# Two transformer blocks on one core: loads, norms and splits placed beside the stage before

## The chip, the core and the metric

The kernel runs on one core of one Trainium2 chip. TensorE (PE) multiplies, with its weight loads shown as PEld; VectorE (DVE), ScalarE (ACT) and GpSimd (POOL) do the elementwise work; SP issues most DMAs, POOL some. The metric is the device time of one execution in microseconds.

## What is computed

The reference takes x of [1, 2048, 1024] in float32 through two blocks.

- Block 1: norm, one input projection, a Fourier branch and grouped-query attention over 16 meta and 2048 other tokens, an output projection, a residual and a norm.
- Block 2: norm; an input projection to 256 + 128 + 32 + 512 + 512 + 8 columns (the compressed query, the compressed key and value, a rope key, the mLSTM's two streams, its gates); an 8-head attention whose queries, keys and values come from the compressed ones by up-projections, with rotary cos and sin on 32 dimensions; an mLSTM in chunks whose input and forget gates run through scans over the sequence; an output projection and residual. Then 32 experts of width 256, two per token out of one group, and an embedding term:

```
y = experts(u) ; x = x + w0*y0 + w1*y1
x = x + sigmoid(norm(x) @ w_ple_gate) * (p @ w_ple) ; out = norm(x)
```

## The kernel before

Every product is made in float32 accuracy from two rounded halves: `split` writes hi on ScalarE (line 73, or 76 with a scale) and lo = raw - hi on VectorE (74, 77) or GpSimd, and `mm3` issues three matmuls, hi x hi (line 83), lo x hi (84), hi x lo (85). The instruction order on each engine is fixed when the kernel is built: it follows the order in which the code issues the work, and each engine runs its list in order. SP's queue, too, runs in order: an issue that waits holds all behind it.

The stages are generators: `e.beside(gen)` in one stage runs the next part of another, up to its `yield`, on the other side of the memory (`e.flip` changes sides).

- `phase_d`, `project_out`: out projection of block 1 in 16 tiles of 128 tokens. `post` in it does the norm.
- `phase_e`: input projection of block 2 in 8 groups of 256 tokens. The weights are in two parts, th/tl (424 columns, 8 splits, loads at lines 848 and 849) and fh/fl (1024 columns, 16 splits in `load_split`, 256 KB each, loads at line 710, three buffers `ws`). `prep(g)` loads, norms, transposes (878) and splits the tokens; products go to `pm`, the th ones first.
- `phase_f`: up-projections in 4 groups of 512 tokens. Each group loads cos and sin (`cs`) and its rope key (`kr`), and the next group's inputs (`xf`, in `load`), makes eight products for the queries, stores QNT and QRT, four for the keys (KNT) and four for the values (V). `put` copies results out of PSUM. `gates` (from line 1380 on) is called at its start: `ig`, `fg` loaded, a chain of VectorE instructions, columns stored to memory and loaded back in another shape (COL, DC), and three transposes on PE at its end.
- `phase_k`: 32 experts. `block(x, second)` is built twice behind a test of the expert's count: with a second pass (`hidden2`, over 64 rows) or without. `hidden` makes eight steps of gate and up products into `g`, one PSUM tile; at each step `beside(k)` puts other work in. `out_a` transposes the activations of the expert before, sg, into ah and al, `out_b` multiplies them by the down weights dh/dl and scatters y to memory. RG and RD are the raw tiles of the up and gate, and of the down weights; `split_in` and `split_down` make halves for expert x + 3 and load the raw tiles again.
- `embed`: the product of p with w_ple (wq, and xq for p), stored as PP, for 13 tiles earlier and, here, for the last 3.
- `phase_l`: the last stage: for 16 tiles load x, yy (two expert results) and pp, add, norm, gate product `pg`, sigmoid, norm, store. The gate's weights lie raw in `raw[0]`, `raw[1]` (2 MB each) and are split to wgh/wgl when the experts are done.

Of the kernel before, what the change touches and what calls it, by code (L numbers as in the profile page):

```python
# [10 lines left out]
F32 = mybir.dt.float32  # L11
# [781 lines left out]
def phase_d(e):  # L793

    nc, d = e.nc, e.d
    MIXT = e.scratch("MIXT", [1024, S])
    X1 = e.scratch("X1", [S, D])

    def post(wk, sm, pt, gb):
        def run(t, r, y):  # L800
            if t == 16:
                return
            ss = sm.tile([128, 1], F32, name="ss")
            junk = wk.tile([128, D], BF, name="junk", bufs=1)
            nc.scalar.activation(junk, y, AF.Square, accum_out=ss)
            rstd(e, sm, ss, D)
            nc.vector.scalar_tensor_tensor(y, y, ss, gb, op0=ALU.mult, op1=ALU.mult)
            nc.sync.dma_start(X1[r, :], y)
        return run

    yield from project_out(e, MIXT, d["w_out"][0], d["x"][0], d["final_g"], "d_", post, False)


def phase_e(e, then):

# [10 lines left out]
    with ExitStack() as st:  # L826
# [3 lines left out]
        ut = pool("e_ut", 2)  # L830
        wk = pool("e_wk", 2)
        wt = pool("e_wt", 1)
        sm = pool("e_sm", 4)
        wp = pool("e_w", 1)
        pt = pool("e_pt", 2, space=PSUM)
        pm = pool("e_pm", 3, space=PSUM)
# [14 lines left out]
        fh, fl = load_split(e, wp, ld, w_in, 1024, 1024, "f", gcol, 416)  # L851
# [3 lines left out]
        taps = cst.tile([128, 4, 5], F32, name="taps")  # L855
        for k in range(4):
            nc.sync.dma_start(taps[:, :, k], d["conv_w_2"][0, k].rearrange("(h p) -> p h", p=128))
        nc.sync.dma_start(taps[:, :, 4], d["conv_b_2"][0].rearrange("(h p) -> p h", p=128))
        xms = [cst.tile([128, 4, 3 + GB], F32, name=f"xm{i}") for i in range(2)]
        nc.gpsimd.memset(xms[0][:, :, :3], 0.0)  # L860

        def prep(g):
            hi = ut.tile([128, 8, GB], F32R, name="uhi")
            lo = ut.tile([128, 8, GB], F32R, name="ulo")
            for i in range(GB // 128):
                t = g * (GB // 128) + i
                xt = ld.tile([128, D], F32, name="xt", bufs=2)
                nc.sync.dma_start(xt, X1[t * 128:(t + 1) * 128, :])
                ss = sm.tile([128, 1], F32, name="ss")
                junk = wk.tile([128, D], BF, name="junk", bufs=1)  # L870
# [11 lines left out]
        prep(0)  # L882
        pend = []

# [15 lines left out]
        for g in range(NG):  # L900
# [5 lines left out]
            for i in range(GB // 128):  # L906
# [6 lines left out]
                junk = wk.tile([128, D], BF, name="junk", bufs=1)  # L913
# [80 lines left out]
def phase_f(e, then):  # L994
# [16 lines left out]
    with ExitStack() as st:  # L1011
# [38 lines left out]
        yield  # L1050
        gates(e, pool)
        xp.append(pool("f_x1", 1))
        ld = pool("f_ld", 2)
        wk = pool("f_wk", 2)
        ps = pool("f_ps", 6, space=PSUM)
        e.stage = ld
        for g in range(S // GB):
            c = slice(g * GB, (g + 1) * GB)
            cs = ld.tile([128, 2, GB], F32, name="cs")
            for i, T in enumerate((CT, ST)):  # L1060
                nc.sync.dma_start(cs[:, i, :], bass.AP(tensor=T.tensor, offset=T.offset + g * GB, ap=[[0, 4], [S, 32], [1, GB]]))
            kr = ld.tile([64, GB], F32, name="kr")
            nc.sync.dma_start(kr, KRW[:, c])
# [7 lines left out]
            nc.sync.dma_start(KRT[:, c], ko[:, 0])  # L1071
# [25 lines left out]
            nc.sync.dma_start(rows(QRT), r)  # L1097
            e.beside(then)
# [801 lines left out]
def embed(e, tiles, side, late=None):  # L1900
# [7 lines left out]
    with ExitStack() as st:  # L1908
# [26 lines left out]
        yield  # L1935
# [13 lines left out]
        x = turn(tiles[0])  # L1949
        for t in tiles:  # L1950
            if t + 3 in tiles:
                load(t + 3)
            (h, l), x = x, turn(t + 1) if t + 1 in tiles else None
            y = wk.tile([128, D], F32, name="y")
            for j in range(2):
                o = slice(j * 512, (j + 1) * 512)
                q = pm.tile([128, 512], F32, name="q", bufs=2)
                for k in range(2):
                    mm3(e, q, (h[:, k], l[:, k]), (w[0][:, k, o], w[1][:, k, o]), k == 0, k == 1)
                nc.scalar.activation(y[:, o], q, AF.Copy)  # L1960
            nc.sync.dma_start(PP[t * 128:(t + 1) * 128, :], y)
            yield
# [23 lines left out]
def phase_k(e, last):  # L1986
# [11 lines left out]
    with ExitStack() as st:  # L1998
# [4 lines left out]
        std, op = far("k_sd", 1), far("k_y", 2)  # L2003
# [21 lines left out]

        def split_in(w, s, x):
# [200 lines left out]
        def block(x, second):  # L2227
# [4 lines left out]
            if x:  # L2232
                a = out_a(SG[x - 1])
# [4 lines left out]
            a2 = []  # L2238

            def beside(k):  # L2240
                if k in TURN and x < 31:
# [36 lines left out]
TURN, OUT2, TURN2 = (0, 2), 6, (4, 5)  # L2278


def phase_l(e, tiles):
# [11 lines left out]
    with ExitStack() as st:  # L2293
# [5 lines left out]
        wq = wp.tile([128, 2, 1024], F32, name="wq")  # L2299
        nc.sync.dma_start(wq, d["w_ple_2"][0].rearrange("(k p) c -> p k c", p=128))  # L2300
        xq = wp.tile([128, len(tiles), 256], F32, name="xq")
        nc.sync.dma_start(xq, d["p_2"][0, 0, tiles.start * 128:tiles.stop * 128].rearrange("(t p) c -> p t c", p=128))
        e.late = wq, xq
# [13 lines left out]
        wg = next(parts)  # L2317
        for _ in parts:
            yield
        ld = pool("l_ld", 2)  # L2320
        wk = pool("l_wk", 2)
# [4 lines left out]
        def head(t):  # L2326
# [3 lines left out]
            if x is None:  # L2330
                x = ld.tile([128, D], F32, name="x", bufs=4)
# [27 lines left out]
        for t in range(16):  # L2359
# [3 lines left out]
            pp = ld.tile([128, D], F32, name="pp")  # L2363
# [10 lines left out]
            sg = wk.tile([128, D], F32, name="sg")  # L2374
# [15 lines left out]
def body(e):  # L2390
    tc = e.tc
    with tc.tile_pool(name="consts", bufs=1) as cp:
# [9 lines left out]
        for _ in phase_d(e):  # L2402
            pass
        e.flip()
        with ExitStack() as st:
# [5 lines left out]
            phase_e(e, heads)  # L2411
# [10 lines left out]
            last = phase_l(e, range(LATE, 16))  # L2422
            phase_k(e, last)
            rest = embed(e, range(LATE, 16), "left", e.late)
            e.beside(rest)
            next(last)
            e.flip()
            for _ in rest:
                pass
            e.flip()  # L2430
# [25 lines left out]
```

## Time and profile before

| what | value |
|---|---|
| median of 3 runs | 3594.97 us (3589.45 to 3596.04) |
| the profiled execution | 3607.51 us, of which its span 3605.8 us |
| mean granted clock of PE | 0.966 |
| PE busy | 3364.2 us (93%), 16556 matmuls |
| VectorE, ScalarE, GpSimd busy | 2448.4, 2052.4, 696.2 us |
| bytes moved | 468.82 MB, 130 GB/s |

The stages around the change, by the first and last matmul of each in the trace:

| stage | from, to (us) |
|---|---|
| out projection of block 1 (`phase_d`) | 1337 to 1529.5 |
| input projection of block 2 (`phase_e`) | 1529.5 to 1827.8 |
| up-projections and gates (`phase_f`) | 1827.8 to 1928.5 |
| experts (`phase_k`) | 2893 to 3374 |
| last stage (`phase_l`) | 3400.6 to 3606 |

Blocks of an expert with a second pass follow one another at 16.2 us, those without (eight of them, 3026 to 3130) at 13.

The profile is one execution on the hardware. A row of the timeline names the engine, the line of the kernel, the tile written and the tiles read, and in square brackets how long the engine stood before it and what ended that. A row of the waits says which engine stood before which line, and for what. [...]

### The profile page before, as it was taken

To read this page: it belongs to the slowest core of one execution; us is meant where nothing else is said; L and a number is where in the kernel's file an instruction comes from. 1 tells how busy PE (TensorE), PEld (TensorE's weight loads), DVE (VectorE), ACT (ScalarE), POOL (GpSimd) and SP (SyncE) were. 2 spreads that over 40 slices of the span, in tenths; PEclk is the share of its full clock that TensorE was granted. 3 is DMA by queue.
4 is the path that set the end of the run, shared out by engine and by line. 5 is a ranking of instruction groups with operands and counts; after the bars stand their busy time and mean duration, and the time that the engine had idled before them with its cause. 6 is when DMAs were issued, how large, how long until landed. Compare 5 with 4: busy or idle time off the path is not lost. (4 is left out here: it accounts for less than half of the span.)

```text
span 3605.8 us, 48799 instructions
## 1 busy us (share of the span) xinstructions
PE 3364.2 (93%) x16556; PEld 2611.3 (72%) x16557; DVE 2448.4 (68%) x4612; ACT 2052.4 (57%) x3660; POOL 696.2 (19%) x729
## 2 busy tenths in 40 slices
PE   8999999999999999989986889989999989899798
PEld 6787766666666657789975667777788766677587
DVE  5835667888888854464365777877856568878554
ACT  4442357887777872253223777877833367677433
POOL 0000000000000010000032333332200046665332
PEclk9999999999999999999997999999999989899899
DMA  5333322111112035353247433322355678888753
GB/s 157 102 121 101 97 70 72 46 31 50 43 32 57 11 91 179 121 153 109 74 148 173 93 77 74 81 69 59 88 174 157 222 260 305 319 301 307 256 189 132
DMA packets 313432, 468.82 MB, mean 130 GB/s; under 512 B 66263, under 2 KB 201192, under 8 KB 304864
## 3 DMA queue, kind: packets, MB, share of 16 engines
q1 hardware_dynamic: 293622, 404.26, 36.9%
q0 software_dynamic: 19520, 60.97, 4.6%
q8 instruction: 148, 2.42, 0.3%
q14 instruction: 142, 1.16, 0.1%
HBM read 333.81 MB, written 135.24 MB: 130 GB/s over the span
## 5 line engine op out<-in xcount | busy, mean ns | idle before, releaser
L588 DVE TENSOR_TENSOR pl<-pe,ph 128x1024 fp32r<-128x1024 f32 (+1 forms) x272 | 340.6, 1253 | 89.0 <-ACT ph L581 87.7
L519 DVE TENSOR_REDUCE mx<-pmx 128x1 f32<-128x512 f32 x512 | 344.2, 684 | 82.9 <-PE pmx L518 76.5
L579 ACT ACTIVATE pe<-ps 128x1024 f32<-128x1024 f32 (+1 forms) x272 | 278.5, 1025 | 146.2 <-PE ps L577 135.9
L581 ACT ACTIVATE ph<-pe 128x1024 fp32r<-128x1024 f32 (+1 forms) x272 | 287.4, 1058 | 7.4
L74 DVE TENSOR_TENSOR gl<-raw,gh 128x512 fp32r<-128x512 f32 x256 | 235.2, 960 | 15.0 <-ACT gh L73 12.6
L576 PE MATMUL ps<-t,kh 128*128 128x512 f32 (+1 forms) x544 | 239.0, 439 | 0.5 <-ACT pe L579 0.5
L1280 DVE TENSOR_TENSOR pl<-pe,ph 128x512 fp32r<-128x512 f32 (+1 forms) x320 | 210.7, 662 | 40.5 <-ACT ph L1273 38.0
L577 PE MATMUL ps<-t,kl 65*128 65x512 f32 (+1 forms) x544 | 222.3, 409 | 0.0
L602 PE MATMUL acc<-ph,vh 128*65 128x512 f32 (+1 forms) x544 | 217.1, 399 | 0.0
L604 PE MATMUL acc<-pl,vh 128*65 128x512 f32 (+1 forms) x544 | 214.9, 395 | 0.0
L603 PE MATMUL acc<-ph,vl 128*65 128x512 f32 (+1 forms) x544 | 214.7, 395 | 0.0
L518 PE MATMUL pmx<-kh,t 128*128 128x512 f32 x512 | 207.1, 410 | 1.9 <-DVE mx L519 1.1
L1244 DVE TENSOR_REDUCE mx<-pmx 128x1 f32<-128x512 f32 (+2 forms) x320 | 190.7, 598 | 13.0 <-PE pmx L1243 12.6
L1271 ACT ACTIVATE pe<-ps 128x512 f32<-128x512 f32 (+1 forms) x320 | 166.9, 524 | 43.5 <-PE ps L1269 40.5
L74 POOL TENSOR_TENSOR dl<-sd,dh 128x512 fp32r<-128x512 f32 x128 | 172.8, 1371 | 71.6 <-ACT dh L73 69.2
L1273 ACT ACTIVATE ph<-pe 128x512 fp32r<-128x512 f32 (+1 forms) x320 | 179.5, 564 | 6.5
L1267 PE MATMUL ps<-t,kh 113*128 113x512 f32 (+1 forms) x320 | 138.0, 431 | 38.8 <-ACT pe L1271 29.8
L73 ACT ACTIVATE gh<-raw 128x512 fp32r<-128x512 f32 x256 | 143.4, 625 | 12.4 <-PE p L85 9.4
L83 PE MATMUL pm<-uhi,fh 128*128 128x256 f32 x512 | 145.3, 285 | 3.7 <-ACT fh L76 2.0
L84 PE MATMUL pm<-ulo,fh 128*128 128x256 f32 x512 | 143.6, 282 | 0.0
L85 PE MATMUL pm<-uhi,fl 128*128 128x256 f32 x512 | 143.2, 283 | 0.3 <-DVE fl L77 0.3
L788 DVE TENSOR_TENSOR y<-p,xt 128x1024 f32<-128x1024 f32 x32 | 39.2, 1224 | 152.9 <-PE p L85 151.2
(539 smaller groups left out, 9672.9 us busy)
## 6 DMA issues: line engine op xcount, KB each, us to landing
raw<-in_w_gate_e SPq DMA_DIRECT2D x32, 1024.0 KB
raw<-in_w_up_e SPq DMA_DIRECT2D x32, 1024.0 KB
sd<-in_w_down_e SPq DMA_DIRECT2D x32, 1024.0 KB
ws<-in_w_in SPq DMA_DIRECT2D x80, 256.0 KB
xt<-in_x SPq DMA_DIRECT2D x32, 512.0 KB
scr_X<-y SPq DMA_DIRECT2D x32, 512.0 KB
xt<-scr_X SPq DMA_DIRECT2D x32, 512.0 KB
yy<-scr_Y POOLq DMA_DIRECT2D x32, 512.0 KB, 5.0
```

Source lines behind the costliest of these rows:

```text
L74: (eng or nc.vector).tensor_tensor(lo, src, f32(hi), op=ALU.subtract)
L518: nc.tensor.matmul(p, t1[:, i * 128:(i + 1) * 128], kh[:, j * 512:(j + 1) * 512], start=True, stop=True)
L519: nc.vector.reduce_max(mx[:, i, j:j + 1], p, axis=AX.X)
L576: nc.tensor.matmul(p[:n, c], kh[:, k0:k0 + n], t1[:, c], start=True, stop=False)
L577: nc.tensor.matmul(p[:n, c], kl[:, k0:k0 + n], t2[:, c], start=False, stop=True)
L579: nc.scalar.activation(pe[:n], p[:n], AF.Exp, scale=0.125)
L581: nc.scalar.activation(ph[:n], pe[:n], AF.Copy)
L588: nc.vector.tensor_tensor(pl[:n], pe[:n], f32(ph[:n]), op=ALU.subtract)
L602: nc.tensor.matmul(A[u][j], vh[:n, i, :65], ph[:n, c], start=i == 0, stop=False)
L603: nc.tensor.matmul(A[u][j], vl[:n, i, :65], ph[:n, c], start=False, stop=False)
L604: nc.tensor.matmul(A[u][j], vh[:n, i, :65], pl[:n, c], start=False, stop=i == 16)
L1280: nc.vector.tensor_tensor(pl[:, c0:], pe[:, c0:], f32(ph[:, c0:]), op=ALU.subtract)
```

## The change

It has four parts.

1. `phase_e` becomes a generator, and its first part (th/tl, the loads, norm, transposes and splits of group 0) is run beside `phase_d` from its tile 13 on (`NEXT`); its loads stand among the first tiles. The fh/fl weights, the taps and the memory they need come behind it.
2. `phase_f` loads cos and sin for all 2048 tokens (`cst`) and the rope key (`krw`) once, in 18 DMAs, ahead of `gates`. The three buffers of `wk` become more (2 to 3), `put` gives VectorE the first of four results and ScalarE three, and KRT is stored behind QRT.
3. In `phase_k`, `out_a` of the expert before moves from the block's start to hidden's step 4 (`OUT`), the second pass' from step 6 to 7, its token transposes from 4 and 5 to 3 and 6.
4. The raw weights of the late `embed` are loaded into the down weights' raw tiles when their last use is done (`load_late`), and no longer into a tile of `phase_l`. `embed` makes its first transposes ahead of its `yield`. In `phase_l`, x, pp and sg lie in quarters of the gate's raw tiles.

```diff
-def phase_d(e):
+def phase_d(e, then):
         def run(t, r, y):
+            if t == NEXT:
+                e.beside(then)
...
+NEXT = 13
 def phase_e(e, then):
-        ut = pool("e_ut", 2)
+        ut = [pool("e_u0", 1)]
...
-        fh, fl = load_split(e, wp, ld, w_in, 1024, 1024, "f", gcol, 416)
...
         prep(0)
+        yield
+        wp = pool("e_w", 1)
+        ut.append(pool("e_u1", 1))
+        wk = pool("e_wk", 2)
+        pm = pool("e_pm", 3, space=PSUM)
+        fh, fl = load_split(e, wp, ld, w_in, 1024, 1024, "f", gcol, 416)
+        taps = wp.tile([128, 4, 5], F32, name="taps")
...
 def phase_f
+        cst = wt.tile([128, 2, S], F32, name="cst")
+        krw = wt.tile([64, S], F32, name="krw")
+        for c in (slice(0, GB), slice(GB, S)):
+            for r in range(4):
+                for i, T in enumerate((CT, ST)):
+                    nc.sync.dma_start(cst[r * 32:(r + 1) * 32, i, c], T[:, c])
+            nc.sync.dma_start(krw[:, c], KRW[:, c])
         gates(e, pool)
-        wk = pool("f_wk", 2)
+        wk = pool("f_wk", 3)
         for g in range(S // GB):
-            cs = ld.tile([128, 2, GB], F32, name="cs")
-            for i, T in enumerate((CT, ST)):
-                nc.sync.dma_start(cs[:, i, :], bass.AP(tensor=T.tensor, offset=T.offset + g * GB, ap=[[0, 4], [S, 32], [1, GB]]))
-            kr = ld.tile([64, GB], F32, name="kr")
-            nc.sync.dma_start(kr, KRW[:, c])
+            cs, kr = cst[:, :, c], krw[:, c]
-            nc.sync.dma_start(KRT[:, c], ko[:, 0])
             def put(o, p, i):
-                if i % 2:
+                if i:
...
             nc.sync.dma_start(rows(QRT), r)
+            nc.sync.dma_start(KRT[:, c], ko[:, 0])
 def embed
-        yield
+        if not late:
+            yield
...
         x = turn(tiles[0])
+        if late:
+            yield
-def phase_k(e, last):
+def phase_k(e, last, keep, tiles):
+        wq = RD[0].rearrange("p (k a) c -> p k (a c)", k=2)
+        xq = RD[1].rearrange("p k c -> p (k c)")[:, :len(tiles) * 256].rearrange("p (t c) -> p t c", c=256)
+        e.late = wq, xq
+        def load_late(i):
...
                     if k == i == 1 and x < 32:
                         load_down(x, s)
+                    elif k == i == 1:
+                        load_late(x % 2)
...
-            if x:
-                a = out_a(SG[x - 1])
             parts(2)
...
             def beside(k):
+                if k == OUT and x:
+                    a.extend(out_a(SG[x - 1]))
-TURN, OUT2, TURN2 = (0, 2), 6, (4, 5)
+OUT, TURN, OUT2, TURN2 = 4, (0, 2), 7, (3, 6)
 def phase_l
-        wq = wp.tile([128, 2, 1024], F32, name="wq")
-        nc.sync.dma_start(wq, d["w_ple_2"][0].rearrange("(k p) c -> p k c", p=128))
...
+        place = [r.rearrange("p (q k) c -> p q (k c)", q=4) for r in raw]
+        xs = [place[0][:, q] for q in range(4)]
+        pps, sgs = ([place[1][:, q] for q in qs] for qs in ((0, 1), (2, 3)))
...
-                x = ld.tile([128, D], F32, name="x", bufs=4)
+                x = xs[t % 4]
-            pp = ld.tile([128, D], F32, name="pp")
+            pp = pps[t % 2]
-            sg = wk.tile([128, D], F32, name="sg")
+            sg = sgs[t % 2]
```

**SP at the start of the up-projections.** Names are those of the code; scr_ marks memory. Before:

```order
L898 DMA scr_GT<-ct 8x128
L1063 DMA kr<-scr_KRW 64x512
L1061 DMA cs<-scr_CT 128x1x512
L1061 DMA cs<-scr_ST 128x1x512
L1398 DMA ig<-scr_GT 64x128
L1399 DMA fg<-scr_GT 64x128
L1063 DMA kr<-scr_KRW 64x512
L1021 DMA xf<-scr_CQNT 128x2x512
L1089 DMA scr_QNT<-o 128x4x512
L1071 DMA scr_KRT<-ko 32x512
L1022 DMA xf<-scr_CKVNT 128x512
```

Now, from the last of the tables' 18 loads on (the other 17, lines 1067 and 1068, stand ahead of these rows):

```order
L1067 DMA cst<-scr_ST 32x1536
L1068 DMA krw<-scr_KRW 64x1536
L1412 DMA ig<-scr_GT 64x128
L1413 DMA fg<-scr_GT 64x128
L1102 DMA scr_QNT<-o 128x4x512
L1110 DMA scr_QRT<-r 128x2x512
L1111 DMA scr_KRT<-ko 32x512
L1119 DMA scr_KNT<-o 128x4x512
```

The loads of the gates' two inputs (ig, fg) moved behind all loads of the tables, and KRT's store behind QRT's.

**ScalarE around the last expert's block.** The rows are those at the branches into and out of the block; wh is the half of the embedding's weights, ah that of the last experts' activations. Before:

```order
L2272 UNCONDITIONAL_BRANCH
L73 ACTIVATE wh<-wq 128x512 x4
L2271 TENSOR_LOAD nb
L2272 COMPARE_AND_BRANCH
L73 ACTIVATE ah<-pt 128x256
L2105 ACTIVATE t_37189<-g_37172 64x512
L2108 ACTIVATE t_37189<-t_37189 64x256
L73 ACTIVATE a_37219<-pt 128x2x64
L2090 ACTIVATE sg<-g_37194 128x256
L2128 ACTIVATE y<-py 128x512
```

Now, from the block's second branch to what stands behind it:

```order
L2304 UNCONDITIONAL_BRANCH
L73 ACTIVATE ah<-pt 128x256
L2122 ACTIVATE sg<-g_37300 128x256
L2160 ACTIVATE y<-py 128x512
L73 ACTIVATE ah<-pt 128x256
L2160 ACTIVATE y<-py 128x512
L2304 UNCONDITIONAL_BRANCH
L76 ACTIVATE wgh<-raw_28433,gcol 128x512 x7
L73 ACTIVATE wh<-sd_28458 128x512 x4
L73 ACTIVATE h<-pt 128x256 x2
```

The four wh splits moved from the block's start, where they stood ahead of ah, to behind seven splits of the gate's weights.

**PE within an expert's block** without a second pass (numbers at names tell the buffers apart). Before, from the block's start:

```order
L2115 MATMUL pt<-ident,sg 128x128 x2
L83 MATMUL g_31106<-gh_28442,xh 128x512
L84 MATMUL g_31106<-gl_28443,xh 128x512
L85 MATMUL g_31106<-gh_28442,xl 128x512
L2061 MATMUL pt<-ident,xr_28504 128x128 x4
```

Now, from behind nine matmuls of hidden on (those are as above):

```order
L2093 MATMUL pt<-ident,xr_28512 128x128 x4
L83 MATMUL g_31107<-gh_28450,xh 128x512
L84 MATMUL g_31107<-gl_28451,xh 128x512
L85 MATMUL g_31107<-gh_28450,xl 128x512
L83 MATMUL g_31107<-gh_28450,xh 128x512
L84 MATMUL g_31107<-gl_28451,xh 128x512
L85 MATMUL g_31107<-gh_28450,xl 128x512
L2147 MATMUL pt<-ident,sg 128x128 x2
L83 MATMUL g_31107<-gh_28450,xh 128x512
```

The two transposes of sg moved from the first place of the block to behind fifteen matmuls of hidden.

## Rows read from the trace of the kernel before

**Rows 1.** Table of stretches: length, busy per engine, granted clock, DMA share, GB/s.

```profile
1530.00:1545.00 15.00, 9.29 (x40) 7.89 (x41) 11.65 (x26) 11.05 (x22) 2.21 (x4) 0.66 0.59 175
1545.00:1560.00 15.00, 12.51 (x66) 10.93 (x65) 11.49 (x32) 12.10 (x29) 1.91 (x3) 0.89 0.75 229
1560.00:1585.00 25.00, 21.26 (x168) 20.17 (x167) 19.54 (x44) 15.00 (x28) 0.86 (x1) 1.00 0.71 204
1830.00:1845.00 15.00, 14.44 (x51) 11.77 (x52) 12.07 (x9) 2.48 (x3) 11.12 (x6) 0.78 0.50 151
...
1860.00:1935.00 75.00, 52.39 (x198) 38.91 (x197) 40.93 (x76) 17.17 (x32) 15.12 (x19) 0.89 0.66 184
...
3026.00:3130.00 104.00, 85.78 (x387) 68.96 (x386) 92.11 (x111) 72.89 (x141) 67.00 (x51) 0.89 0.91 332
3130.00:3350.00 220.00, 208.42 (x999) 158.66 (x997) 175.31 (x257) 165.02 (x321) 132.28 (x106) 1.00 0.80 298
3350.00:3370.00 20.00, 11.01 (x40) 8.28 (x40) 4.24 (x9) 3.45 (x8) 4.84 (x4) 0.74 0.85 277
3370.00:3410.00 40.00, 23.59 (x91) 17.60 (x90) 26.30 (x37) 19.74 (x36) 13.71 (x20) 0.79 0.71 260
```

**Rows 2.** PE's waits, 1529 to 1590: us in total, times, longest.

```profile
PE pm L83 <- ACT th L76: 2.9, 2, 2.6
```

**Rows 3.** Groups by line, 1530 to 1585: count, busy, mean ns.

```profile
L77 DVE SCALAR_TENSOR_TENSOR fl<-ws,gcol,fh 128x512 fp32r<-128x512 f32 x16 | 11.8, 746 | 3.3 <-ACT fh L76 3.2
```

**Rows 4.** Waits of all engines, 1860 to 1930.

```profile
POOL ko L1068 <- DMA kr<-scr_KRW: 26.3, 1, 26.3
...
PE p L83 <- ACT o L1081: 13.8, 4, 7.2
ACT o L1081 <- DMA scr_KNT<-o: 13.5, 3, 9.5
```

**Rows 5.** SP's queue in order of time, 1825 to 1930: start, us, what.

```profile
1829.25 0.52 SPq L1061 DMA_DIRECT2D cs<-scr_CT  x1
...
1838.05 0.49 SPq L1398 DMA_DIRECT2D ig<-scr_GT  x1
...
1889.88 0.60 SPq L1021 DMA_DIRECT2D xf<-scr_CQNT  x1
...
1895.16 0.60 SPq L1459 DMA_DIRECT2D scr_DC<-dm  x1
```

**Rows 6.** PE's waits, 2920 to 3350.

```profile
PE pt L2115 <- DVE sg L2091: 20.2, 7, 4.5
PE pt L2115 <- DVE y L2149: 8.6, 15, 0.6
```

**Rows 7.** VectorE's groups by shape, 3026 to 3130.

```profile
L74 DVE TENSOR_TENSOR gl<-raw,gh 128x512 fp32r<-128x512 f32 x63 | 68.6, 1124 | 3.9 <-ACT gh L73 3.6
L74 DVE TENSOR_TENSOR xl<-pt,xh 128x512 fp32r<-128x512 f32 x16 | 10.9, 679 | 1.2 <-ACT xh L73 1.2
```

**Rows 8.** Waits of all engines, 3350 to 3412.

```profile
POOL scr_Y L2052 <- DVE al L74: 16.5, 1, 16.5
...
ACT wh L73 <- DMA wq<-in_w_ple: 12.2, 1, 12.2
...
PE py L83 <- ACT ah L73: 8.9, 2, 8.4
...
ACT junk L2340 <- DMA scr_PP<-y: 5.9, 1, 5.9
```

**Rows 9.** VectorE in order of time, 3370 to 3392: start, us, what.

```profile
3374.71 4.73 DVE L77 SCALAR_TENSOR_TENSOR wgl<-raw,gcol,wgh 128x512 fp32r<-128x512 f32 x7 [0.19 <-ACT wgh L76]
...
3387.03 1.28 DVE L2337 SCALAR_TENSOR_TENSOR x<-yy,wt,x 128x1024 f32<-128x1024 f32 x1 [2.35 <-DMA yy<-scr_Y]
```

**Rows 10.** GpSimd in order of time, 3376 to 3384.

```profile
3379.56 2.11 POOL L2335 DMA_DIRECT2D yy<-scr_Y  x4 [0.90 <-DMA scr_Y<-y,dst]
```

**Rows 11.** PE in order of time, 3398 to 3402.

```profile
3400.58 0.80 PE L83 MATMUL pg<-wgh,hh 128*128 128x512 f32 x1 [5.89 <-ACT hh L73]
```

More of the change, by code (lines that the diff above doesn't have):

```diff
@@ L854, in phase_e @@
         NG = S // GB
[L855 to L860, printed above, removed]
         def prep(g):
-            hi = ut.tile([128, 8, GB], F32R, name="uhi")
-            lo = ut.tile([128, 8, GB], F32R, name="ulo")
+            hi = ut[g % 2].tile([128, 8, GB], F32R, name="uhi")
+            lo = ut[g % 2].tile([128, 8, GB], F32R, name="ulo")
             for i in range(GB // 128):
@@ L869, in prep @@
                 ss = sm.tile([128, 1], F32, name="ss")
-                junk = wk.tile([128, D], BF, name="junk", bufs=1)
+                junk = ld.tile([128, D], BF, name="junk", bufs=1)
                 nc.scalar.activation(junk, xt, AF.Square, accum_out=ss)
@@ L882, in phase_e @@
         prep(0)
+        yield
[5 more added lines that the diff above has]
+        taps = wp.tile([128, 4, 5], F32, name="taps")
+        for k in range(4):
+            nc.sync.dma_start(taps[:, :, k], d["conv_w_2"][0, k].rearrange("(h p) -> p h", p=128))
+        nc.sync.dma_start(taps[:, :, 4], d["conv_b_2"][0].rearrange("(h p) -> p h", p=128))
+        xms = [wp.tile([128, 4, 3 + GB], F32, name=f"xm{i}") for i in range(2)]
+        nc.gpsimd.memset(xms[0][:, :, :3], 0.0)
         pend = []
@@ L912, in phase_e @@
                 ss = sm.tile([128, 2], F32, name="ss2")
-                junk = wk.tile([128, D], BF, name="junk", bufs=1)
+                junk = ld.tile([128, D], BF, name="junk", bufs=1)
                 nc.scalar.activation(junk[:, :256], p[:, :256], AF.Square, accum_out=ss[:, 0:1])
@@ L2001, in phase_k @@
         far = lambda n, b: st.enter_context(e.pool(n, b, side="left" if e.side == "right" else "right"))
-        std, op = far("k_sd", 1), far("k_y", 2)
+        std = keep.enter_context(e.pool("k_sd", 1, side="left" if e.side == "right" else "right"))
+        op = far("k_y", 2)
         slots = [early.enter_context(e.pool("k_w0", 1)), far("k_w1", 1)]
@@ L2024, in load_down @@
             nc.sync.dma_start(s.rearrange("p (k a) c -> p k (a c)", k=2), d["w_down_e_2"][0, x].rearrange("(k p) c -> p k c", p=128))
+        wq = RD[0].rearrange("p (k a) c -> p k (a c)", k=2)
+        xq = RD[1].rearrange("p k c -> p (k c)")[:, :len(tiles) * 256].rearrange("p (t c) -> p t c", c=256)
+        e.late = wq, xq
+        def load_late(i):
+            if i == 0:
+                nc.sync.dma_start(wq, d["w_ple_2"][0].rearrange("(k p) c -> p k c", p=128))
+            else:
+                nc.sync.dma_start(xq, d["p_2"][0, 0, tiles.start * 128:tiles.stop * 128].rearrange("(t p) c -> p t c", p=128))
         def split_in(w, s, x):
@@ L2275, in phase_k, with phase_l @@
                 block(x, False)
-TURN, OUT2, TURN2 = (0, 2), 6, (4, 5)
-def phase_l(e, tiles):
+OUT, TURN, OUT2, TURN2 = 4, (0, 2), 7, (3, 6)
+def phase_l(e):
     nc, tc, d = e.nc, e.tc, e.d
@@ L2401, in body @@
             pass
-        for _ in phase_d(e):
-            pass
-        e.flip()
         with ExitStack() as st:
@@ L2410, in body @@
             heads = phase_f(e, latent)
-            phase_e(e, heads)
+            second = phase_e(e, heads)
+            for _ in phase_d(e, second):
+                pass
+            e.flip()
+            for _ in second:
+                pass
             for rest in (heads, latent, out):
@@ L2421, in body @@
             e.flip()
[L2422 to L2430, printed above, removed]
+            last = phase_l(e)
+            with ExitStack() as keep:
+                phase_k(e, last, keep, range(LATE, 16))
+                rest = embed(e, range(LATE, 16), "left", e.late)
+                e.beside(rest)
+                next(last)
+                e.flip()
+                for _ in rest:
+                    pass
+                e.flip()
             for _ in last:
```

11 lines of the change are left out of this document (3 added, 8 removed).

## The prediction

> **What bounds the kernel now.** TensorE (PE) is the bound almost everywhere, so I first look for the stretches in which it is not. The table of stretches [rows 1] gives, for each, its length, PE's busy time and the granted clock. Three losses stand out. In 1530 to 1585, behind the first block's out projection, PE is busy 9.29 + 12.51 + 21.26 = 43.1 of 55 us, and for the first 15 us its clock is 0.66. In 1860 to 1935, the MLA up-projections, it is busy 52.4 of 75 at 0.89. In 3350 to 3410, between the last expert and the gate product, it is busy 11.0 + 23.6 = 34.6 of 60 at 0.74 and 0.79. The expert loop is two things: 3026 to 3130 runs with PE 85.8 of 104 busy and VectorE (DVE) 92.1, and the 220 us after it with PE 208.4 busy. [...] Then I ask, stretch by stretch, which wait ends last. The profiled execution took 3607.5 us, 12.5 above the median of 3595.0. I make the sum against the 3607.5 and take 12.5 off at the end.
>
> **A, the second block's start beside the out projection.** The eight th/tl splits and their loads, the norm and transposes of the first 256 tokens move beside the last tiles of the projection. Before, these stand behind the projection's last matmul. PE waits 2.9 us for th alone [rows 2], and DVE can begin the sixteen fl splits only after the eight tl splits. Nothing is added: the same 16 transposes, 8 + 8 splits and 16 loads; they lie beside an out projection in which VectorE and ScalarE have room. In 1530 to 1585 PE stands 11.9 us and the clock costs 9.29 x 0.34 + 12.51 x 0.11 = 4.5, together 16.4 us that could be had. What is late next is fl: 16 splits at 0.75 us of VectorE [rows 3], each behind a 256 KB load that waits for one of three buffers. The order puts the first fl split behind the projection's last output, some 7 us after its last matmul; the 48 th matmuls (0.4 us long, pipelined to about half) and the 8 or more transposes cover only the first 10 us. The first eight fl splits at 1.4 us each (28 us for 16 before, with other work between) end about 18 us after the last matmul, so PE stands again some 6 to 8 us. I take 16.4 - 6.4 = **-10**, bounds -16 (all) and -4 (fl takes the place of th). The loads that move to the projection's first tiles, 1.9 MB, and the SP queue that they stand in, lie beside tiles whose loads come one tile ahead; I cost that at nothing, up to 2 us if that cover is gone. The taps' five loads move behind fl and lie between its loads on SP; that is inside the 1.4 us.
>
> **B, tables of cos and sin.** Twelve loads inside the four groups become 18 at the start, ahead of the gates' loads. What goes: GpSimd's (POOL) ko waiting 26.3 us for kr [rows 4], which stood behind the gates' chain in SP's order, and with it some of the waits of the products. The third buffer for o takes away waits like ScalarE's 13.5 us for the stores of KNT, while PE itself lost 13.8 us to ScalarE's o. In 1860 to 1935 PE stands 22.6 us, and the clock costs 52.4 x 0.11 = 5.8: 28 us are the ceiling. What comes: the gates' ig load left at 1838.05 [rows 5]; now nine more issues of 0.52 us, as that of cs, stand before it (+5 us), and VectorE's first gates' instruction stands behind a rope product of the second group (+10 us more). The whole chain moves with it, and its end matters: its last store, DC, left at 1895.16. The load of group 3's input was issued before DC (1889.88); now it stands behind it on SP, and behind SP wait all later stores and loads. The chain's slow part does not depend on the tables (column stores of 64 x 4 B, about 6 us each by the gap from one to the next). So group 3 waits for the end of the chain and starts 73 to 78 us after the second block's in-projection, and with its 16 us and what follows the stage ends at 90 to 96, against 100.7 before. I take **-5**; bounds -15 (chain as early as before, half of the ceiling) and +8 (chain late by the whole 15 us, less the 7 that it had to spare).
>
> [...] The trace moved 151 GB/s in 1830 to 1845, at half of the engines' time [rows 1]. At that rate the 2.6 MB of tables take 17 us, and the input of group 1 with the gates' two loads land behind them: chain late by about 10 more, B = +8, the sum 13 us higher. [...]
>
> **C, the expert loop.** Transposes of the former expert's activations move from the block's start to behind hidden's fifth step, and two others by a step. Nothing is added. PE waited at the block's start 20.2 us for sg (7 times) and 8.6 for y (15 times at 0.57) [rows 6]. In blocks with a second pass (16.2 us long, PE-bound) the 0.57 us go, up to 8.6 in all, if nothing else is late. In the eight blocks of 3026 to 3130 the 20 us do not go: the next hidden product writes the PSUM tile that sg's multiplication reads, so PE waits for the same instruction, only at a matmul instead of a transpose. What may come: al, the low half that the down product needs, was second on VectorE in a block and now stands behind six gl (1.124 us) and two xl (0.68) [rows 7], 6 x 1.124 + 2 x 0.68 = 8.1 us; PE reaches the down product after 24 hidden matmuls and 10 transposes, some 7 us at full clock in a block without a second pass. About 1 us late there, 8 times, but VectorE is the bound in these blocks and goes on with gl meanwhile: half counts. In blocks with a second pass VectorE has 6 to 7 us more. -8.6 + 4 = -4.6, taken as **-5**; bounds -9 and +8 (1 us in each of the eight and a trifle in each other).
>
> **D, the last stage's start.** The embedding's raw weights go to the third product's raw tiles and are loaded two blocks earlier. Before, their load left only when the last block began, and ScalarE waited 12.2 us for it with the last experts' ah queued behind; PE waited 8.9 for that ah, and POOL's scatter 16.5 [rows 8]. Now the wh splits stand behind the last block. Without the 8.4 us wait and its half clock the last py ends near 3363.5 instead of 3373.8 (two down products of 2.8 us, a transpose and a split): -10. From there: the seven wgh/wgl splits (4.7 us, [rows 9]) and then four wh/wl (2.5) stand on VectorE, so the embedding's products start near 3371 and take 8.3 us to about 3380 with the transposes. The scatter lands near 3368 and yy takes 7.5 us (issued at 3379.56 [rows 10], used at 3387.03 [rows 9]), so it is there at 3375.7. VectorE gets to x behind 13.8 us of splits at 3378 (before, 3387.03), has two x and one wgl to do, 3381; transposes 1.8, the norm's square and hh 1.7: the gate product starts at 3384 to 3385. Before it started at 3400.58 [rows 11], delayed too by ScalarE's junk, which waited 5.9 us for a store of PP since its buffer lay where the embedding's had; that wait goes with the new places. 16 us earlier, less a us for the clock: **-15**; bounds -20 (start at 3380) and -5 (only the 8.4 us wait goes, 3 us come back as waits for yy). The tiles of x, pp and sg in the gate's raw tiles cost nothing later: as many buffers as before, and the sixteen steps after 3410 are PE-bound. At the start POOL's queue stands at pp until the last split has read raw; the third yy stood there for VectorE's x anyway.
>
> **Sum.** -10 - 5 - 5 - 15 = -35: 3572.5 on the profile's scale, **3560** on the median's. About 0.2% (7 us) is what a measurement of this kernel can tell from no change: faster is under 3588, slower over 3602.
>
> **Rivals.** (1) The tables' loads crowd the start of the up-projections and the chain ends late: B = +8, the others as above: 3573. For it: the SP order, and POOL and DVE queues that stop at the chain. Against: the DMA engines have half of their time free there. (2) The waits only change places: fl in place of th (-3), nothing in B and C, D only -4 since the last experts' yy still have to come: 3588. For it: three of the four parts leave the last link of their chain as it is. (3) Everything goes to its far end, -16 - 15 - 9 - 20 = -60: 3535. (4) The slow one: al. If VectorE is so far behind in every block that the down product waits for al, PE, the bound, loses that time 32 times. The other parts give 30, so from 0.95 us a block the kernel is slower than before; at 1.5 us it takes 48 - 30 = 18 us more: 3613. For it: al behind 8 us of splits, gl at 1.124 us beside GpSimd's dl. Against: in the blocks with a second pass PE needs 10 us or more to get to the down product.
>
> **How the numbers follow.** Forecast 0.57, (1) 0.16, (2) 0.11, (3) 0.08, (4) 0.08. The range of 3538 to 3590 holds the forecast, (1), (2) and the half of (3) that is nearest, and the parts' bounds taken together; beyond it lie (4) and the rest of (3). Faster: forecast, (1), (3) and some of (2), 0.84; same: most of (2), 0.08; slower: (4), 0.08.
>
> **What would show it.** A: in the 55 us behind the out projection PE stands 4 to 8 us instead of 11.9, the th wait is gone and the new one is fl. B: no wait of ko for kr, ig loaded some 5 us later, group 3's first product at the end of the gates' chain, the stage 5 to 10 us shorter; wrong if DC comes after 1910. C: the 0.57 us waits for y gone, the waits for sg still about 20 us but at the hidden product; wrong if py waits for al over 0.5 us a block. D: no wait for wq, the gate product 15 us earlier after the last expert. What would break the sum is C above all: it alone is repeated 32 times.

## The result, and the profile after

The changed kernel takes **3559.2 us** in the median of four runs (3557.5 to 3560.1) against 3592.2 for the kernel before on the same chip: a ratio of 0.9899, interval 0.9883 to 0.9916. 3560 was forecast. In a second comparison on another chip the ratio was 0.9903 (0.9884 to 0.9921). The size was right: a gain of 35 us was forecast, 33 were measured (36 by the ratio). The parts came out less well, two of them for another reason than was given, so that the close agreement is partly luck.

The two profiled executions differ by 47 us of span (3605.8 and 3558.4), more than the medians. A second profile of the kernel before (below, label w_before) shows where most of the excess lies: its stretch between the up-projections and the second out projection, whose code the change leaves alone, took 678.0 us, and 691.3 in the first profile. So single differences between two executions are read with care here, and the stages are compared over all profiles. They run from matmul to matmul:

| stage (us) | before, two profiles | after, two profiles |
|---|---|---|
| out projection of block 1 | 189.2, 189.4 | 191.4, 191.4 |
| its end to the second token group of the in-projection | 57.1, 58.2 | 41.1, 41.7 |
| last token group to the first up-projection | 36.3, 36.3 | 41.8, 43.1 |
| up-projections | 98.3, 96.8 | 93.4, 92.8 |
| MLA attention and mLSTM | 691.3, 678.0 | 674.0, 681.7 |
| experts up to the last hidden product | 457.7, 456.0 | 452.4, 452.2 |
| from there to the last down product | 17.3, 18.0 | 6.5, 6.5 |
| from there to the first gate product | 26.8, 28.9 | 28.7, 28.8 |
| gate product's stage | 192.6, 190.9 | 190.0, 191.3 |

The table of stretches of the changed kernel, columns as in [rows 1], the granted clock as a share of full speed: the start of the second block, the up-projections, the experts and the end.

```profile
1530.00:1545.00 15.00, 14.73 (x89) 13.74 (x88) 11.32 (x27) 9.43 (x24) 0.70 (x1) 1.00 0.66 186
1545.00:1560.00 15.00, 14.55 (x117) 13.97 (x117) 13.82 (x38) 11.63 (x21) 1.93 (x3) 1.00 0.76 217
1560.00:1585.00 25.00, 21.56 (x149) 20.55 (x148) 12.12 (x34) 10.90 (x31) 0.97 (x2) 1.00 0.43 137
1820.00:1835.00 15.00, 14.06 (x68) 11.62 (x67) 5.75 (x9) 3.81 (x6) 1.78 (x4) 1.00 0.61 165
...
1850.00:1925.00 75.00, 48.85 (x187) 36.45 (x188) 38.92 (x74) 21.86 (x41) 17.52 (x21) 0.84 0.67 196
2996.00:3100.00 104.00, 89.83 (x415) 69.35 (x414) 85.77 (x115) 77.26 (x151) 67.49 (x55) 0.95 0.92 351
```

Against [rows 1]: in the 55 us behind the out projection PE is busy 50.8 instead of 43.1 at a clock of 1.00 throughout, so the slow start, at a mean clock of 0.66, is gone. In the experts' slow stretch the clock is 0.95 instead of 0.89 and PE busy 89.8 of 104 instead of 85.8. In the up-projections PE still stands 26 of the 75 us.

What PE waits for from 1529 to 1590 in the changed kernel, as in [rows 2] (us in total, times, longest): the wait for th is gone.

```profile
PE pm L83 <- ACT ev L956: 2.4, 2, 1.5
PE pm L83 <- ACT fh L76: 1.1, 1, 1.1
PE pt L875 <- DVE ulo L74: 0.3, 1, 0.3
PE pm L85 <- DVE fl L77: 0.3, 1, 0.3
```

And SP's queue in the changed kernel's up-projections, as in [rows 5]. The in-projection's last product ends at 1820.8 here, against 1827.3 before.

```profile
1835.61 0.59 SPq L1412 DMA_DIRECT2D ig<-scr_GT  x1
...
1882.79 0.59 SPq L1473 DMA_DIRECT2D scr_DC<-dm  x1
1883.42 0.59 SPq L1030 DMA_DIRECT2D xf<-scr_CQNT  x1
```

### The profile page after: what moved, and what is told of

Its sections match the earlier page's. It is cut to its first block, busy times and chain, and to the rows that moved or that the text cites. A ratio compares the mean times of both kernels' runs of the same rounds, so it can differ in the third digit from the quotient of the medians.

```text
span 3558.4 us, 48779 instructions
## 1 busy us (share of the span) xinstructions
PE 3340.2 (94%) x16556; PEld 2592.6 (73%) x16557; DVE 2427.9 (68%) x4600; ACT 2052.8 (58%) x3672; POOL 688.9 (19%) x729
## 5 line engine op out<-in xcount | busy, mean ns | idle before, releaser
L74 DVE TENSOR_TENSOR gl<-raw,gh 128x512 fp32r<-128x512 f32 x256 | 222.1, 915 | 19.0 <-ACT gh L73 18.6
L74 POOL TENSOR_TENSOR dl<-sd,dh 128x512 fp32r<-128x512 f32 x128 | 165.4, 1313 | 80.4 <-ACT dh L73 77.8
L1281 PE MATMUL ps<-t,kh 113*128 113x512 f32 (+1 forms) x320 | 136.0, 425 | 35.7 <-ACT pe L1285 28.9
L626 POOL TENSOR_TENSOR rc<-rc,ag 128x512 f32<-128x512 f32 x16 | 23.9, 1495 | 608.0 <-DMA rc<-scr_RD 561.6
```

Source lines behind the costliest of these rows:

```text
L74: (eng or nc.vector).tensor_tensor(lo, src, f32(hi), op=ALU.subtract)
```

## The four parts, each undone

Each of these kernels is the changed one with one part as before; a short diff names the edit.

**Part A undone.**

```diff
-def phase_d(e, then):
+def phase_d(e):
-            if t == NEXT:
-                e.beside(then)
```

with `phase_e`'s pools and its fh/fl loads as before.

> The changed kernel with part A undone (nothing of the second block runs beside the out projection). By the two traces, A brings the second token group of the in-projection 14.3 us forward, but in the last group 6.6 us are lost again while VectorE and GpSimd run memsets of the next attention's key tiles; the stage as a whole is 6 us earlier. Theory: these memsets came early because of A's memory, so undoing A costs 6 us against the changed kernel (about 3565). Rival: the memsets came early for another reason (B's tables), then undoing A costs its gross 12 to 14 us (about 3572).

Measured: 3574.7 us, ratio 0.9927 (0.9915 to 0.9940), some 9 us over the changed kernel's 0.9899 and 0.9903. The memsets stand behind the in-projection again, so they came early through A, as the theory had it; the cost lies between the two figures. The stages show why it is above 6: undoing A makes the last group 36.3 us again (41.8 with A), but the second group starts 57.3 us after the out projection (41.1), and the up-projections, into which the memsets return, take 97.2 (93.4 and 92.8), no less than the 98.3 and 96.8 of the kernel before: B, which this kernel has, shortens that stage only beside A. The gates' chain shows it: its last store, DC, leaves 67.7 us after the in-projection's last product here, 62.0 in the changed kernel. The out projection itself took 185.0 us, 4 to 6 less than with A.

**Part B undone.** Its edit is the diff of `phase_f` above, backwards.

> The changed kernel with part B undone (cos, sin and rope key loaded per group, two o buffers, copies shared evenly). Theory: the up-projections are 7 us longer again (about 3566), and the wait of 12 us for group 3's inputs behind the gates' chain goes back to several smaller waits. Rival: the early memsets in the in-projection's last group are B's doing; then undoing B gives 6.6 us back there and the kernel stays within 2 us of the changed one.

Measured: 3571.5 us, ratio 0.9915 (0.9901 to 0.9929). The up-projections took 104.1 us, against 93.4 and 92.8 with B, and 98.3 and 96.8 in the kernel before, so A alone makes this stage longer; why isn't shown. The rival falls: the last group of the in-projection stays at 40.4 us, the memsets are not B's. The interval reaches to the changed kernel's ratio, so the 11 us of the stage carry this verdict, not the total.

**Part C undone.**

```diff
-OUT, TURN, OUT2, TURN2 = 4, (0, 2), 7, (3, 6)
+TURN, OUT2, TURN2 = (0, 2), 6, (4, 5)
```

with `a = out_a(SG[x - 1])` at the block's start.

> The changed kernel with part C undone (the former expert's transposes at a block's start again). By the traces the loop up to the last block is 6 us shorter, of which only 3 are PE waits and the rest a clock that falls less. Theory: 5 to 6 us slower than the changed kernel (about 3565), PE waiting some 30 us for sg and y at the block's start. Rival: the new waits for al (9.8 us) and xl (15.9 us) eat what the old ones cost, the difference is within 2 us.

Measured: 3571.7 us, ratio 0.9917 (0.9904 to 0.9930); the loop 459.5 us against 452.4 and 452.2. PE's waits in the loop of this kernel, and then in the changed one's (us in total, times, longest):

```profile
PE pt L2147 <- DVE sg L2123: 19.9, 7, 4.5
PE pt L2147 <- DVE y L2181: 11.5, 16, 2.0
PE pt L2168 <- DVE t L2141: 3.5, 2, 2.6
```

```profile
PE pt L2147 <- DVE xl L74: 15.9, 12, 1.9
PE py L85 <- DVE al L74: 9.8, 7, 2.2
PE g L83 <- DVE y L2181: 2.3, 4, 0.6
PE pt L2168 <- DVE t L2141: 2.2, 3, 1.7
```

The first is [rows 6] again. With the change the transposes' waits for sg and y are gone (2.3 us for y are left at hidden's product), and two others have come, for xl (the buffers of the transposes) and for al. All of PE's waits in the loop are 34 instead of 38 us; many short ones in place of seven long ones. The clock of the slow stretch is 0.90 here and 0.95 with the change. As with B, the interval reaches to the changed kernel's, and the stage carries the verdict: the loop took 459.5 us here, 457.7 and 456.0 before, and 451.5 to 455.6 in all ten other profiles with C.

**Part D undone.** The weights wq and xq load into tiles of `phase_l`, x, pp and sg lie in pools.

> The changed kernel with part D undone (the embedding's weights loaded in the last block, the last stage's tiles in memory of their own). Theory: the last block is 10 us longer again, the start of the gate product follows the last down product 2 us sooner than now, so 8 to 10 us slower than the changed kernel (about 3568). Rival: what ends last is the chain scatter, yy, x, which is as long in both; then D's 16 us, as predicted, would all be lost (about 3575).

Measured: 3576.1 us, ratio 0.9935 (0.9921 to 0.9949), 12 us over the changed kernel. From the last hidden product to the last down product it takes 16.1 us again (6.5), then 27.6 to the gate product (28.7). The rival, a chain as long in both, falls for the first link and holds for the second. The waits of the end, of this kernel and of the changed one:

```profile
POOL scr_Y L2066 <- DVE al L74: 14.4, 1, 14.4
...
ACT wh L73 <- DMA wq<-in_w_ple: 9.9, 1, 9.9
...
PE py L83 <- ACT ah L73: 8.2, 2, 7.6
```

```profile
PE q L83 <- ACT h L73: 10.8, 1, 10.8
...
ACT y L1977 <- DMA scr_PP<-y: 6.0, 1, 6.0
...
POOL scr_Y L2084 <- DMA scr_Y<-y,dst: 5.5, 1, 5.5
...
ACT wh L73 <- DMA scr_Y<-y,dst: 5.3, 1, 5.3
```

The load of yy, which brings the experts' results to the last stage, in the changed kernel (as in [rows 10]):

```profile
3336.91 2.20 POOL L2366 DMA_DIRECT2D yy<-scr_Y  x4 [3.72 <-DMA scr_Y<-y,dst]
```

The wait for wq goes, as forecast. In its place wh waits for a scatter's landing, since the embedding's tiles lie where the experts' outputs do, and the third output waits for a store of PP. The last scatter, too, is now issued later after the last down product, 5.1 us (2.1 before), and so is the load of yy, 9.9 us (5.8 before).

Against the mean ratio of the changed kernel, 0.9901, the four parts cost 9, 5, 6 and 12 us, together 32 of its 36. With intervals of some 5 us to either side that agrees with parts that add, but doesn't show it, and in the up-projections A and B do not add: 98.3 and 96.8 us with neither, 97.2 with B alone, 104.1 with A alone, 93.4 and 92.8 with both. The totals by themselves show A and D; B and C rest on their stages.

## What the new waits cost

**The changed kernel again.**

> The changed kernel again, on the chip of the runs of this call, so that they can be compared with it. Both theories: ratio near 0.990 to the kernel before.

Measured: 3563.3 us, ratio 0.9903. Its second profile is the one in the table above.

**The output tiles elsewhere.**

```diff
-        op = far("k_y", 2)
         slots = [early.enter_context(e.pool("k_w0", 1)), far("k_w1", 1)]
+        op = far("k_y", 2)
```

> The changed kernel with the pool of the experts' output tiles (y, y2) laid behind the pool of the weights' halves, so that the embedding's wh and wl lie where hidden's weights lay and not where y waits for its scatter. Theory: ScalarE's wait of 5.3 us for a scatter's landing ahead of wh goes, the embedding's products start 5 us earlier, and the gate product too: 4 to 5 us faster than the changed kernel. Rival: the start of the gate product hangs on the chain of the last two scatters, yy and x, which is as before: within 1 us, and PE only stands later.

Measured: ratio 0.9901 (0.9883 to 0.9919), the same. wh no longer waits, PE's q no longer stands 10.8 us, but the gate product comes 26.9 us after the last down product, against 28.7 and 28.8: the rival is nearer, and the next waits, for a PP store (4.7 us) and for hh (8.0), take most of it.

**The xm tiles in the first part's pool.**

```diff
-        xms = [wp.tile([128, 4, 3 + GB], F32, name=f"xm{i}") for i in range(2)]
+        xms = [cst.tile([128, 4, 3 + 256], F32, name=f"xm{i}") for i in range(2)]
```

> The changed kernel with the in-projection's xm tiles in the pool of its first part again, which holds that memory until its last group is done, so that the memsets and selects of the next attention's key tiles come behind it. Theory: the in-projection's last group gets its 6.6 us back (34.7 instead of 41 us), the up-projections lose 3 to 4 us to the memsets: 3 us faster than the changed kernel. Rival: the memsets cost the same wherever they run, since the up-projections wait for VectorE too: within 1 us.

Measured: ratio 0.9892 (0.9874 to 0.9911); alone not to be told from the changed kernel. The stages do tell: last group 36.0 us (41.8 and 43.1), up-projections 96.1 (93.4 and 92.8), as the theory had both. Why the memsets cost so much there is seen on VectorE's convolution products (ev) of that group. The groups of the changed kernel, then of this one:

```profile
L952 DVE SCALAR_TENSOR_TENSOR ev<-xm,taps,ev 128x256 f32<-128x256 f32 x12 | 10.4, 876 | 0.2
L1170 DVE CAST kl<-ones 1x2048 fp32r<-1x2048 f32 x2 | 4.0, 2010 | 0.1
L1164 DVE MEMSET kh<- 113x2048 f32 x2 | 3.5, 1765 | 0.8 <-DMA scr_KRW<-ct 0.4 <-issue 0.4
```

```profile
L952 DVE SCALAR_TENSOR_TENSOR ev<-xm,taps,ev 128x256 f32<-128x256 f32 x12 | 5.8, 485 | 3.1 <-ACT ev L950 2.8
```

876 ns each instead of 485, since three of the twelve last about four times as long, and these lie beside GpSimd's selects (VectorE and then GpSimd in order of time, changed kernel):

```profile
1795.97 2.80 DVE L1170 CAST kl<-ones 1x2048 fp32r<-1x2048 f32 x1
...
1798.80 2.00 DVE L952 SCALAR_TENSOR_TENSOR ev<-xm,taps,ev 128x256 f32<-128x256 f32 x1
1800.73 0.41 DVE L948 COPY xm<-pm 128x256 f32<-128x256 f32 x1
1801.06 0.47 DVE L952 SCALAR_TENSOR_TENSOR ev<-xm,taps,ev 128x256 f32<-128x256 f32 x1
...
1805.92 0.41 DVE L948 COPY xm<-pm 128x256 f32<-128x256 f32 x1
1806.26 1.77 DVE L952 SCALAR_TENSOR_TENSOR ev<-xm,taps,ev 128x256 f32<-128x256 f32 x1
1808.06 1.22 DVE L1170 CAST kl<-ones 1x2048 fp32r<-1x2048 f32 x1
```

```profile
1795.79 4.74 POOL L1166 TENSOR_SCALAR_AFFINE_SELECT kh<-kh 113x2048 fp32r<-113x2048 f32 x2 [3.37 <-DVE kh L1164]
1803.83 3.93 POOL L1166 TENSOR_SCALAR_AFFINE_SELECT kh<-kh 113x2048 fp32r<-113x2048 f32 x2 [3.30 <-DVE kh L1164]
```

The product of 2.00 us ends at 1800.8, as the first pair of selects does (1800.5); the next one, without them, takes 0.47. The product of 1.77 us ends at 1808.0, as the second pair does (1807.8). A cast of kl beside the selects takes 2.80 us, and 1.22 behind them. PE then waits 5.2 us for xm and ev in this group, which it did not before.

**Both, and three buffers for the embedding's outputs.**

```diff
-            y = wk.tile([128, D], F32, name="y")
+            y = wk.tile([128, D], F32, name="y", bufs=3 if late else None)
```

> The two former edits together, and three instead of two buffers for the embedding's last outputs, so that the third product's copy doesn't wait 6 us for a store. Theory: the effects add, the gate product starts 7 us sooner after the last down product, the whole 8 to 10 us faster than the changed kernel. Rival: x from the scatters comes last, so only the in-projection's 3 us are left.

Measured: 3558.8 us, ratio 0.9892 (0.9875 to 0.9909), less than was hoped in the total and still within the changed kernel's interval. By the stages the effects do add: 23.3 us to the gate product (28.8), last group 36.2, up-projections 93.5.

**The tables alone taken out.** Cos, sin and rope key per group again, the rest of B kept.

```diff
-            cs, kr = cst[:, :, c], krw[:, c]
+            cs = ld.tile([128, 2, GB], F32, name="cs")
```

> The changed kernel with part B undone in one respect: cos, sin and rope key are loaded per group again, with three buffers for o, the copies of results and the place of KRT's store as changed. Theory: the tables are what counts, the up-projections take 101 to 104 us as with all of B undone, 7 us slower than the changed kernel. Rival: the buffers and copies count, the stage stays near 94 us and the time within 2 us.

Measured: 3567.1 us, ratio 0.9921 (0.9908 to 0.9935). The stage took 93.3 us: the tables do nothing for it, and the rival is right there. But the total is by the ratio 7 us over the changed kernel's, not within 2. The intervals overlap, so the total doesn't decide this alone; the stages tell where the time goes: the next one opens later. Counted by its fortieth product for a maximum (pmx), which started 72.6 us after the up-projections here, 70.6 and 70.9 before, 69.0 with all of B undone, and 64.7 to 68.2 in the nine profiles with tables (66.7 and 68.0 in the changed kernel's), the tables are worth some 5 us there beside the rest of B; with all of B undone the stage opens only 1 to 2 us later. The rope key's store shows why. SP's queue in this kernel and in the changed one:

```profile
1870.21 0.54 SPq L1469 DMA_DIRECT2D scr_DC<-dm  x1
...
1919.14 0.33 SPq L1107 DMA_DIRECT2D scr_KRT<-ko  x1
1920.41 0.37 SPq L1106 DMA_DIRECT2D scr_QRT<-r  x1
1920.83 0.46 SPq L1177 DMA_DIRECT2D kf<-scr_KRT  x1
```

```profile
1912.16 0.36 SPq L1110 DMA_DIRECT2D scr_QRT<-r  x1
1912.57 0.46 SPq L1111 DMA_DIRECT2D scr_KRT<-ko  x1
1913.12 0.76 SPq L1179 DMA_DIRECT2D kf<-scr_KNT  x1
1913.93 0.59 SPq L1181 DMA_DIRECT2D kf<-scr_KRT  x1
```

With the tables the last rope key is stored 3 us before the stage's end (1915.6), without them 4.6 after it (1914.5), and the attention that reads it starts behind. The first row shows that the tables do crowd the gates' chain: without them its last store, DC, leaves 50.4 us after the in-projection's last product (1819.85), with them 62.0. The stage is as short all the same.

**Group 3's inputs from another queue.** The three edits above, and

```diff
+            q = nc.scalar if g == 3 else nc.sync
-            nc.sync.dma_start(xf[:, 2, :], CKN[:, c])
+            q.dma_start(xf[:, 2, :], CKN[:, c])
```

for both loads of xf.

> The three edits of the former call together (output tiles' place, xm tiles' place, three buffers for the embedding's outputs), and group 3's inputs in the up-projections loaded from ScalarE's queue and not from SP's, where they stand behind the gates' chain. Theory: PE's wait of 10 to 12 us ahead of group 3 goes for the most part, the stage is 6 to 8 us shorter than with the three edits alone (86 to 88 us), the whole 12 us faster than the changed kernel. Rival: PE then waits for the gates' transposes, which stand ahead of group 3 in its order: the stage shortens by under 2 us.

Measured: **3545.8 us** against 3595.1 before, ratio 0.9867 (0.9852 to 0.9882), below the kernel before, and just clear of the changed kernel (0.9883 at the least). Of the 12 us ahead of group 3's first product (the changed kernel's row, then this one's) nothing is left:

```profile
1896.12 2.07 PE L83 MATMUL p<-xh,wqh 128*128 128x512 f32 x4 [11.99 <-ACT xh L73]
```

```profile
1882.70 0.79 PE L83 MATMUL p<-xh,wqh 128*128 128x512 f32 x1
```

The stage is 90.0 us (93.5 with the three edits), longer than the theory's 86 to 88: ScalarE's and VectorE's copies now wait for the stores of QNT (11.6 and 9.7 us), and PE behind them, 9.6 us in pieces. The rival falls: PE waits 0.4 us for the gates' transposes. The ratio lies some 9 us below that of the three edits, of which the stage shows 3.5; the two intervals overlap, so what this last edit is worth in the total stays open.

**The kernel before again.**

> The kernel before once more, for a second profile. The first took 12 us over its median, and the stretch from the end of the up-projections to the second out projection was 691 us in it, against 674 to 682 in eight profiles of kernels that leave its code alone. Theory: that stretch is 675 to 682 us here, so the 17 us by which it shrank from before to after in the first comparison are mostly spread between executions. Rival: it is 690 again; then the change shortens it, by what starts earlier beside it.

Measured: 3587.0 us; the stretch in question 678.0 us, as the theory had it. The first profile of before was an execution with a long one; why that stretch varies isn't shown.

## Why the prediction was right, point by point

The forecast came out within 1 us of the median, but not every step held: in A two errors offset each other, B's gain has another reason than was given, and D gained too little. That the sum came so close is partly luck. That the kernel is faster is not: each part undone makes the change worth less, in its stage or in the total.

- **A, -10: right in the sum by two errors that cancel.** Both gains are there: PE stands 4.2 us instead of 11.9, and the second group starts 16 us sooner. The prediction held 6.4 of these 16.4 us back for fl as the new wait, and that hardly came: PE waits 1.1 us for fh and 0.3 for fl, less than for ev (2.4 us, 1.7 and 2.3 before). The eighth fl split did end late, as forecast (18.5 us after the out projection's last matmul); PE had other work. What the prediction did not see is that the tiles which A moves to the other pool free memory in which the next attention's memsets and selects then run, within the in-projection's last group; that takes some 6 of the 16 back, by chance about what was held back for fl. That the loads lie beside the out projection at no cost isn't settled: it took 191.4 us twice, 189.1 to 190.0 in eight other kernels with A, 185.0 in the one without, but 189.2 and 189.4 before. The 4.5 us that its sum gives to the clock, busy time times what the clock lacks, are an estimate that no run shows by itself. The trace of before shows 128x424 products of the in-projection every 0.35 us at a granted clock of 0.50 (1539.4 to 1542.6) and every 0.19 at 1.00 (1546 to 1552).
- **B, -5: right in size, wrong in its reason.** The times came as forecast: the gates' chain ends the wait for group 3 (12 us, behind DC on SP), whose first product starts 75.3 us after the in-projection's last (73 to 78 forecast; 71.8 before), and the stage ends at 94.8 (90 to 96; 101.5 before). The 15 us by which the chain was to end later did not come: DC left 62.0 us after the in-projection's last product, 67.8 before, though ig left 14.8 us after it instead of 10.7. So the chain ended no later, and the rival of the crowded start falls. But the tables do lengthen the chain (62.0 us with, 50.4 without them), and A shortens it: with A undone DC leaves at 67.7. The step that failed is the one that gave the gain to the tables: without them the stage is as short. The copies, the third buffer and the order of the stores shorten it together; which of them does most, no run shows. By the kernel without them, the tables gain some 5 us at the start of the next stage, which the prediction did not look at. One sign was missed: ko still waits 12.3 us for krw (26.3 for kr before), at no cost that shows. DMA at the start moved 165 GB/s in 1820 to 1835, hardly over the 151 of [rows 1], and 237 in 1832 to 1836, with the tables' loads alone. That the tables would load faster than at 151, on which the choice of -5 over the +8 worked out at that rate hung, no row of before showed; it was the author's estimate.
- **C, -5: right in size, one step wrong.** The wait for y went. The wait for sg was to stay at 20 us at another place; it went, and shorter ones for xl and al came in its place. That al would be late is so: 9.8 us in seven blocks, 1.4 us each, where 1 us in eight blocks was forecast. It is not so in every block, and the slow rival falls. PE's waits fell by only 4 us in sum; the rest of the gain goes with a clock of 0.95 instead of 0.90 in the slow stretch, which the prediction did not have among its terms.
- **D, -15: too much by 3 to 6.** The first step held: the last block is 11 us shorter. The second, 5 us more up to the gate product, failed, and nothing came of it. The prediction had 21 us from the last down product to the gate product (3363.5 to 3384.5); it took 28.7. It had the wh splits start at once behind the gate's, and they wait 5.3 us for a scatter. It counted the wait of junk as gone; the store moved its wait to the third output. It also had the scatter landed 4.5 us after the last down product; the last one was only issued 5.1 us after it, and yy 9.9. The wait for wh alone was not the cause, since its removal gave 1.9 us; with both waits gone it was 23.3 us, 5.4 less.

## What to carry to other kernels

Whoever moves work into a pool that is opened earlier changes which memory comes free when: follow what is laid there next, since a later stage's memsets can start in the middle of a busy one. Small edits can be worth as much as large ones: a third buffer and moved output tiles gave 5.4 us ahead of the gate product, the queue of a single load 3.5 us in its stage, the reordering of a whole loop some 5. Forecast each part of such an edit by itself, too: B's tables and its third buffer had one price between them, and it went to the wrong one. And a stage's gain may stand at the start of the next one, so each edit is measured up to the point at which the work after it runs as before.

## What the runs showed of the hardware

- Beside GpSimd's four selects of kh (1.89 to 2.77 us each), three of VectorE's twelve products of xm and ev, both tiles in SBUF, took 2.00, 2.12 and 1.77 us, the other nine 0.36 to 0.80. Each of the three ended 0.3 us after a select did, while a copy out of PSUM (xm from pm) beside the last select took 0.41. The cast of kl took 2.80 us beside the selects instead of 1.22 behind them. What ties these instructions to the selects no run shows. By these rows, the selects of this kernel are best placed where VectorE has none of them: behind the products, in v_xm, ev took 485 ns each instead of 876.
- While loads of cs, each four copies of 32 rows in one DMA, ran in the kernel before, the mean busy share of the DMA engines was 0.27 (columns as in [rows 1]):

```profile
1833.00:1834.00 1.00, 1.00 (x4) 0.81 (x3) 0.94 (x2) 0.00 (x0) 1.00 (x1) 0.50 0.27 100
```

  That is 100 GB/s. While the tables' loads alone ran in the changed one (1832 to 1836; each of cos and sin has 32 rows), the view gives a share of 1.03 at 237 GB/s. No run changes the shape of the loads alone, so what of this comes from it isn't shown. B's size does not come from it, since the stage is as short without the tables (93.3 us; 93.4 and 92.8 with them).
- The stretch of MLA attention and mLSTM took 674 to 691 us over the thirteen profiles of the kernels told of here; its code is the same in all of them, though in those without the tables it opens later. Between the two executions of the kernel before alone that is 13 us, as much as the largest part of the change is worth. Other stages vary less: the gate product's 190.0 to 192.6 us, the out projection 185.0 (A undone) to 191.4.
